# Sixteen gate column blocks moved behind the mLSTM into a segment of their own, in a one-core streaming-encoder layer

## The chip, the core and the metric

The kernel runs on one core of one Trainium2 chip. The metric is device microseconds of one execution. The kernel before took 1607.51 us (median of 3 runs, 1606.27 to 1607.71).

## The reference

One trunk layer of a hybrid encoder, for a prompt of 1024 tokens and a sample stream of 32 tokens (1056 token columns together), all in float32. What matters here, shortened:

```python
h = rmsnorm(x, g_mix) * (1 + sc1) + sh1
u = h @ w_in                                   # 1024 x 5640
qa, ka, va, qm, km, vm, om, ip, fp, ga, gm = split(u)
ya = band_attention(qa, ka, va, rel_bias)      # 8 heads x 64, own 64-frame chunk and 8 before it
q_m, k_m = silu(causal_conv4(qm, km))
hm = mlstm_chunkwise(q_m, k_m, vm, ip, fp)     # 4 heads x 128, running matrix memory
ym = head_rmsnorm(hm) * sigmoid(om)
merged = sigmoid(ga) * (ya @ w_br_att) + sigmoid(gm) * (ym @ w_br_mlstm)
x = x + gt1 * (merged @ w_out)
x = x + gt2 * ((silu(g) * up) @ w_down)        # after a second modulated norm
```

The merge gates `ga` and `gm` are 2 x 1024 columns of the one input projection. They are used first in the merge, after both branches are done.

## The kernel before

**The products.** TensorE holds a 128x128 block of weights and streams token columns. The 1056 columns are cut in three tiles of 352. A product of float32 accuracy is made of three passes (`PASSES`): weights and activations are each split into a high and a low part. So one 128-column block of `w_in` over one tile (`unit`, L458) is 8 k-blocks times 3 passes, 24 matmuls of 128x352, and a block of three tiles is 72. Each weight block comes by DMA (512 KB, `wraw`), ACT copies its high part (L424) and POOL or DVE subtracts for the low part (L425): POOL as long as the second mLSTM has not begun, DVE from then on (`hm_n[1]` in `weight`).

**The blocks of the input projection** are the `segs` list, worked through in order: for each of four head pairs a key, a value and a query block (`b_qkv`), then the mLSTM's values and convolution inputs (`vm_block`, `conv_block`), its output gates (`om_block`) and the sixteen merge gate blocks (`gate_block`). A gate block is 72 matmuls, three copies out of PSUM on ACT (L677) and one store of 528 KB to a scratch tensor in HBM (`g_d`, L678). The merge reads it back.

**Work beside the blocks.** A segment can name a generator (`attention(hp)`, `mlstm(pr)`, `branch_operands`) that is run beside its blocks. `unit` calls `side.tick()` after every second k-block, so one tick is 6 matmuls and a block of three tiles is 12 ticks. A job started with so many steps and so many ticks takes steps/ticks of a step at each tick; a remainder is drained at the segment's end:

```python
ticks = sum(4 * run.w[2] for run in blocks)
delay = 13 if i >= 5 else 0
job = side.start(gen(), steps, ticks - delay - 4, delay)
```

The order of instructions on TensorE, VectorE (DVE), ScalarE (ACT) and GpSimd (POOL) is the order in which this program writes them; nothing is reordered later. Only SyncE (SP), which issues the DMAs, is ordered by a scheduler.

**One attention step** (`attention`, 22 steps a head pair, one item a step: a head and 128 queries against up to 640 keys): PE transposes the weights of the item before last (L774, into the one `psT` buffer), makes the scores (L747, into the one `psS` buffer) and the values of the item three back (L805, one `psV` buffer for two items). DVE adds the bias and takes the extreme (L761), makes the low part of the transposed weights (L786), the reciprocal (L766) and, after two items, two sums out of `psV` (L812, L813). ACT takes the exponential (L762), copies the transposed weights (L781) and the first value sum (L811). POOL scales the weights (L767). The first step of head pairs 1 to 3 makes the low parts of the queries on DVE (`low_queries`, L643).

**One mLSTM iteration** is two steps (`first` and `second`, 9 blocks of tokens for two heads): PE's scores and transposes (L1107, L1109), its products with the memory, for the memory and for the output (L1137, L1140, L1142). On DVE: `scaled` (L1171), `weigh` (L1125), the memory update (L1151), the sum (L1154), three small ones (L1158 to L1160), and the decay weights (L1113). ACT squares (L1163), POOL takes the root (L1165, L1166), and `scaled` of the next iteration needs that root.

**A second job**, `ada_rest`, runs beside all segments from the second on: 160 steps over 495 ticks, most of them one DVE instruction of 128x512 (L1229).

Of the kernel before, what the change touches and what calls it, by code (L numbers as in the profile page):

```python
# [139 lines left out]
def hybrid_stream_step(  # L140
# [37 lines left out]
    def slot(shape, dt=F32):  # L178
        return slots.tile(shape, dt, tag="s", name=nm("s"))

    def tmpt(shape=(P, T), dt=F32):
        return tmp.tile(list(shape), dt, tag="t", name=nm("t"))

    def mmt():
        return mm.tile([P, 512], F32, tag="mm", name=nm("mm"))
# [236 lines left out]
    def split_to(dst, src, eng=dve):  # L422

        act.activation(dst[:, 0], src, AF.Copy)  # L424
        eng.tensor_tensor(dst[:, 1], src, f(dst[:, 0]), op=ALU.subtract)  # L425
# [25 lines left out]
    def unit(w, w0, xt, lo, hi, last=True):  # L451

        wt = W.use(w)
        pt = mmt()
        n = len(xt)
        for k in range(n):
            for q, (a, b) in enumerate(PASSES):
                pe.matmul(pt[:, :hi - lo], wt[(w0 + k) // 4][:, a, (w0 + k) % 4], xt[k][:, b, lo:hi],  # L458
                          start=(k == 0 and q == 0), stop=(k == n - 1 and q == 2))
            if k % 2 == 0 and k:  # L460
                side.flush(1)
            if k % 2 == 1:
                side.tick()
        if last:
            W.used(w)
        return pt[:, :hi - lo]
# [86 lines left out]
    def w_cols(c0, home=None):  # L553
        return weight([w_in[:, c0:c0 + P]], KD, 3, home)
# [115 lines left out]
    def gate_block(g, j):  # L670
        w = w_cols((GA, GM)[g] + j * P)

        def run():
            raw = tmpt()
            for lo, hi in TILES:
                pt = unit(w, 0, hs, lo, hi)
                act.activation(raw[:, lo:hi], pt, AF.Copy)  # L677
            sp.dma_start(g_d[2 * j + g], raw)  # L678
        run.w = w
        return run  # L680
# [155 lines left out]
    ATT_STEPS = 22  # L836
# [364 lines left out]
    ML_STEPS = 2 * (NB + 3) + 2  # L1201
# [56 lines left out]
    def om_block(b):  # L1258
        w = w_cols(OM + b * P)

        def run():
            if b % 2 == 0:
                om[b // 2] = slot([P, 2, T])
            for lo, hi in TILES:
                pt = unit(w, 0, hs, lo, hi)
                act.activation(om[b // 2][:, b % 2, lo:hi], pt, AF.Copy)
        run.w = w
        return run

    def branch_operands():  # L1270
        for b in range(4):
            o = om[b // 2][:, b % 2]
            act.activation(o, o, AF.Sigmoid)
            dve.tensor_tensor(o, o, hm_n[b // 2][:, b % 2], op=ALU.mult)
            y = slot([P, 2, T], F32R)
            yield
            split_to(y, o)
            ym.append(y)
            yield
        if "ym" in dbg:  # L1280
            for h in range(MH):
                sp.dma_start(dbg["ym"][h], om[h // 2][:, h % 2])
        for b in range(4):
            raw = tmpt()
            sp.dma_start(raw, ya_d[b])
            y = slot([P, 2, T], F32R)
            split_to(y, raw)
            ya.append(y)
            yield

    BR_STEPS = 12

    def chain(*gens):
        for g in gens:
            yield from g


    def b_qkv(hp):
        return [k_block(hp), v_block(hp), q_block(hp)]
# [3 lines left out]
    def b_gates(a, b):  # L1303
        return [gate_block(g, j) for g, j in gates[a:b]]

    def mix(a, b):

        out = []
        for i, x in enumerate(a):
            out.append(x)  # L1310
            out += b[i * len(b) // len(a):(i + 1) * len(b) // len(a)]
        return out
# [7 lines left out]
    def conv_rows():  # L1320
        yield
        pt = mmt()
        pe.transpose(pt[:48, :P], ncv, ident)
        ncr = tmpt((48, P))
        dve.tensor_copy(ncr, pt[:48, :P])
        sp.dma_start(new_conv_p[0, 0].rearrange("j (r c) -> (j r) c", c=P), ncr[0:24])
        sp.dma_start(new_conv_s[0, 0].rearrange("j (r c) -> (j r) c", c=P), ncr[24:48])

    nothing = lambda: None
    segs = [  # L1330
        (nothing, b_qkv(0), None, 0),
        (nothing, mix(b_qkv(1), b_gates(0, 2)), lambda: attention(0), ATT_STEPS),
        (nothing, mix(b_qkv(2), b_gates(2, 4)), lambda: attention(1), ATT_STEPS),
        (conv_state, b_qkv(3) + b_gates(4, 8), lambda: attention(2), ATT_STEPS),
        (mlstm_setup, [vm_block(0), conv_block(0), conv_block(4), conv_block(1), conv_block(5)],
         lambda: attention(3), ATT_STEPS),
        (open_mls, [vm_block(1), conv_block(2), conv_block(6), conv_block(3), conv_block(7)],
         lambda: mlstm(0), ML_STEPS),
        (nothing, [om_block(b) for b in range(4)] + b_gates(8, 16),
         lambda: chain(mlstm(1), conv_rows(), branch_operands()), ML_STEPS + BR_STEPS + 3),  # L1340
    ]

    for _, blocks, _, _ in segs:
# [431 lines left out]
    for pi, tiles in enumerate(parts):  # L1775
        if pi == 1:
            job = side.start(second_norm(parts[0]), 15, 50)
        for j in range(KD):
# [21 lines left out]
            a, b = tiles[0][0], tiles[-1][1]  # L1800
# [494 lines left out]
```

## Time and profile before

| what | value |
|---|---|
| timed runs | 1606.27, 1607.51, 1607.71 us; median 1607.51 |
| profiled execution | span 1604.4 us (its time outside the span is not listed apart) |
| PE busy | 1576.2 us, 98% of the span |
| PE's weight loads (PEld) | 1554.8 us, 97% |
| DVE, ACT, POOL busy | 1135.5, 786.2, 445.3 us |
| granted TensorE clock | 0.999 |
| `wraw` from `w_in` | 38 DMAs of 512 KB, 4.0 us from issue to landing |
| `g_d` stores | 16 DMAs of 528 KB, 3.9 us |

The page gives busy time by engine, and groups of instructions by source line. Consecutive matmuls overlap in the records, so the distance between starts says more than the length of one. In a list of instructions in order of time a row is: start in us, length in us, engine, line, operation, what it writes and reads, how many instructions the row joins, and in brackets the idle time before it with what ended it. A table by stretches gives each engine's busy us and, in brackets, its instructions. The segments of the kernel before lie in the span about like this: first products to 72 us, first head pair's blocks to 90, then attention of head pair 0 (90 to 171), 1 (171 to 256), 2 (256 to 360) and 3 (360 to 465), the first mLSTM pair (465 to 570), and om blocks, gates 8 to 15, the second mLSTM pair and the branch operands (570 to 720).

### The profile page before, as it was taken

What the parts mean: (1) busy time and instruction counts of PE and PEld (TensorE: products, weight loads), DVE (VectorE), ACT (ScalarE), POOL (GpSimd) and SP (SyncE); (2) the same over time, 40 slices, a digit from 0 to 9 for tenths busy, and PEclk for the clock granted to TensorE, in tenths of its full rate; (3) what the DMA queues carried; (4) which work ended last, traced back from release to release, by engine and by line L of the source; (5) the groups of instructions that cost most, each with busy time, mean ns of one, the idle gap of its engine ahead of it and who ended that gap; (6) DMA issues with size and microseconds to landing.
All of it is one profiled execution on the core that took longest, in us unless ns stands there. A gap on an engine that the chain in (4) does not pass through costs nothing.

```text
span 1604.4 us, 27406 instructions
## 1 busy us (share of the span) xinstructions
PE 1576.2 (98%) x10256; PEld 1554.8 (97%) x10256; DVE 1135.5 (71%) x2185; ACT 786.2 (49%) x1747; POOL 445.3 (28%) x477
## 2 busy tenths in 40 slices
PE   7999999999999999999999999999999999999997
PEld 6989999999999999999999999999999999999997
DVE  7766564646776855556654699988888986799754
ACT  3665463544455644444443655554544444545443
POOL 2344243433332411000012100566565650000001
PEclk9999999999999999999999999999999999999999
DMA  9823323232222232675353311313222227427453
GB/s 362 273 77 91 97 82 102 88 122 86 67 80 80 69 95 69 121 276 168 121 153 113 106 54 48 100 55 105 81 79 94 67 82 252 135 79 250 135 156 126
DMA packets 210414, 192.45 MB, mean 120 GB/s; under 512 B 10706, under 2 KB 180618, under 8 KB 209258
## 3 DMA queue, kind: packets, MB, share of 16 engines
q1 hardware_dynamic: 205386, 187.82, 37.4%
q10 hardware_dynamic: 4640, 2.82, 0.6%
q8 instruction: 81, 1.33, 0.4%
q14 instruction: 51, 0.42, 0.1%
q0 software_dynamic: 256, 0.06, 0.0%
HBM read 152.19 MB, written 41.63 MB: 121 GB/s over the span
## 4 chain that ended last, share of the span: by engine, by line
PE 88%; DVE 5%; DMA 3%; ACT 2%; issue 1%; SPq 0%; ACTq 0%; POOL 0%; DVEq 0%; POOLq 0%
PE mm L458 39%; PE psb L1843 18%; PE mm L1843 10%; PE mm L2246 3%; PE mm L906 3%; PE psb L2246 2%; PE psV L805 2%; PE psb L2089 2%; PE psS L747 1%; DMA s<-in_w_ada_dram 1%; PE psT L774 1%; PE mm L2089 1%; DMA wraw<-in_w_in_dram 1%; DMA t<-in_x_sample_dram 1%; DVE s L390 1%
## 5 line engine op out<-in xcount | busy, mean ns | idle before, releaser
L458 PE MATMUL mm<-s,wsp 128*128 128x352 f32 x4104 | 689.1, 324 | 0.0
L458 PEld LDWEIGHTS mm<-s,wsp 128*128 128x128 f32 x4104 | 656.9, 188 | 2.0 <-issue 0.4
L425 DVE TENSOR_TENSOR wsp<-wraw,wsp 128x512 fp32r<-128x512 f32 (+1 forms) x280 | 234.9, 855 | 120.0 <-ACT wsp L424 118.0
L1843 PE MATMUL psb<-s,wsp 128*128 128x352 f32 x1611 | 271.7, 322 | 1.5 <-DVE wsp L425 0.8
L424 ACT ACTIVATE wsp<-wraw 128x512 fp32r<-128x512 f32 x336 | 199.5, 617 | 141.5 <-PE psb L1843 44.0
L1843 PEld LDWEIGHTS psb<-s,wsp 128*128 128x128 f32 x1611 | 260.6, 188 | 2.1 <-DVE wsp L425 1.1
L1843 PE MATMUL mm<-s,wsp 128*128 128x352 f32 x933 | 159.3, 322 | 0.0
L1843 PEld LDWEIGHTS mm<-s,wsp 128*128 128x128 f32 x933 | 151.2, 188 | 0.5 <-DVE wsp L425 0.5
L767 POOL TENSOR_SCALAR st<-st,mx 128x640 f32<-128x640 f32 (+5 forms) x72 | 55.7, 774 | 184.8 <-DVE mx L766 170.5
L1229 DVE SCALAR_TENSOR_TENSOR t<-wa,cmix,t 128x512 f32<-128x512 f32 x112 | 89.1, 801 | 15.0 <-DMA wa<-in_w_ada_dram 14.6
L425 POOL TENSOR_TENSOR wsp<-wraw,wsp 128x512 fp32r<-128x512 f32 x56 | 75.8, 1374 | 49.4 <-ACT wsp L424 47.9
L762 ACT ACTIVATE st<-st,mx 128x640 f32<-128x640 f32 (+5 forms) x72 | 47.9, 666 | 71.6 <-DVE mx L761 70.3
L761 DVE CUSTOM_DVE_ANT_0 st<-psS,bias 128x640 f32<-128x640 f32 (+5 forms) x72 | 44.3, 616 | 46.1 <-PE psS L747 33.2
L1790 POOL TENSOR_TENSOR t<-t,sl 128x352 f32<-128x352 f32 x19 | 18.3, 961 | 185.3 <-DMA wraw<-in_w_out_dram 130.8
L781 ACT ACTIVATE pT<-psT 128x640 fp32r<-128x640 f32 (+3 forms) x80 | 38.6, 493 | 63.1 <-PE psT L774 47.7
L2158 POOL TENSOR_TENSOR fst<-fst 128x1 f32<-128x1 f32 (+1 forms) x6 | 1.2, 192 | 236.6 <-ACT t L2151 236.6
L786 DVE TENSOR_TENSOR pT<-psT,pT 128x640 fp32r<-128x640 f32 (+3 forms) x80 | 43.9, 557 | 22.5 <-ACT pT L781 22.3
L1452 POOL TENSOR_TENSOR wraw<-wraw,raw 128x512 f32<-128x512 f32 x33 | 55.8, 1702 | 0.9
L906 PE MATMUL mm<-s,s 128*128 128x264 f32 (+3 forms) x432 | 54.8, 283 | 0.0
L2246 PE MATMUL mm<-s,wsp 128*128 128x352 f32 x330 | 54.4, 324 | 0.0
L2246 PEld LDWEIGHTS mm<-s,wsp 128*128 128x128 f32 x330 | 53.1, 188 | 0.0
L1452 POOL TENSOR_TENSOR spare<-wraw 128x512 f32<-128x512 f32 x11 | 16.5, 1496 | 130.0 <-DMA wraw<-in_w_gate_up_dram 122.4
(396 smaller groups left out, 2561.3 us busy)
## 6 DMA issues: line engine op xcount, KB each, us to landing
wraw<-in_w_in_dram SPq DMA_DIRECT2D x38, 512.0 KB, 4.0
wraw<-in_w_gate_up_dram SPq DMA_DIRECT2D x33, 512.0 KB, 3.8
wa<-in_w_ada_dram SPq DMA_DIRECT2D x64, 256.0 KB, 2.9
wraw<-in_w_down_dram SPq DMA_DIRECT2D x32, 512.0 KB, 4.0
a_d<-t SPq DMA_DIRECT2D x22, 528.0 KB, 2.8
g_d<-t SPq DMA_DIRECT2D x16, 528.0 KB, 3.9
x<-xres SPq DMA_DIRECT2D x16, 528.0 KB, 6.7
t<-g_d SPq DMA_DIRECT2D x16, 528.0 KB, 5.4
```

Of the source, the lines that this page charges most:

```text
L424: act.activation(dst[:, 0], src, AF.Copy)
L425: eng.tensor_tensor(dst[:, 1], src, f(dst[:, 0]), op=ALU.subtract)
L458: pe.matmul(pt[:, :hi - lo], wt[(w0 + k) // 4][:, a, (w0 + k) % 4], xt[k][:, b, lo:hi], start=(k == 0 and q == 0), stop=(k == n - 1 and q ...
L761: dve.tensor_tensor_reduce(so, sv, bi, -1.0, 3.0e38, ALU.add, ALU.min, mx[:n, 1:2])
L762: act.activation(st[:n, :w], st[:n, :w], AF.Exp, bias=mx[:n, 1:2], scale=-1.0, accum_out=mx[:n, 2:3])
L767: pool.tensor_scalar(st[:n, :w], st[:n, :w], mx[:n, 3:4], 1.0, op0=ALU.mult, op1=ALU.mult)
L906: pe.matmul(pt[:n, :wd], hs[k][:, a, i * P:i * P + n], whl[b][:, k, :wd], start=(k == 0 and q == 0), stop=(k == KD - 1 and q == 2))
L1229: dve.scalar_tensor_tensor(ac[:, c], wa, cmix[:, c, k:k + 1], ac[:, c], op0=ALU.mult, op1=ALU.add)
L1452: self.eng.tensor_tensor(a(dst), a(x), a(y), op=op)
L1843: pe.matmul(acc, wt[:, a, k], x[k][:, b], start=(start and not onto and k == 0 and q == 0), stop=(stop and k == 3 and q == 2), skip_group_ ...
L2089: pe.matmul(acc, wt[k // 4][:, u, k % 4], piece_of[k, i][:, v], start=(k == 0 and q == 0), stop=(k == KP - 1 and q == 2))
L2246: pe.matmul(acc, wt[(k - k0) // 4][:, u, (k - k0) % 4], piece_of[k, 2][:, v], start=(k == 0 and q == 0), stop=(k == NF - 1 and q == 2))
```

## The change

The gates leave the segments of attention 0, 1 and 2 (two, two and four blocks) and the last segment (eight). A new last segment holds all sixteen, and `branch_operands` runs beside them. Attention 0 to 2 keep their 22 steps but have 36 ticks (three blocks) in place of 60, 60 and 84. The second mLSTM pair and the convolution rows keep their 29 steps but have the 48 ticks of the four om blocks; before, they shared 144 ticks with `branch_operands`. Total ticks are the same, and so is the arithmetic. The weights of the first eight gates are now split on DVE instead of POOL.

```diff
@@ -1329,15 +1329,16 @@
     segs = [
         (nothing, b_qkv(0), None, 0),
-        (nothing, mix(b_qkv(1), b_gates(0, 2)), lambda: attention(0), ATT_STEPS),
-        (nothing, mix(b_qkv(2), b_gates(2, 4)), lambda: attention(1), ATT_STEPS),
-        (conv_state, b_qkv(3) + b_gates(4, 8), lambda: attention(2), ATT_STEPS),
+        (nothing, b_qkv(1), lambda: attention(0), ATT_STEPS),
+        (nothing, b_qkv(2), lambda: attention(1), ATT_STEPS),
+        (conv_state, b_qkv(3), lambda: attention(2), ATT_STEPS),
         (mlstm_setup, [vm_block(0), conv_block(0), conv_block(4), conv_block(1), conv_block(5)],
          lambda: attention(3), ATT_STEPS),
         (open_mls, [vm_block(1), conv_block(2), conv_block(6), conv_block(3), conv_block(7)],
          lambda: mlstm(0), ML_STEPS),
-        (nothing, [om_block(b) for b in range(4)] + b_gates(8, 16),
-         lambda: chain(mlstm(1), conv_rows(), branch_operands()), ML_STEPS + BR_STEPS + 3),
+        (nothing, [om_block(b) for b in range(4)] + b_gates(0, 0),
+         lambda: chain(mlstm(1), conv_rows()), ML_STEPS + 3),
+        (nothing, b_gates(0, 16), branch_operands, BR_STEPS),
     ]
```

How this moves instructions, at the two places of which the prediction speaks. First PE in attention of head pair 0, second head, full width (640 keys), in the kernel before. `st` are the weights to transpose, `s_699` the keys, `mm` is the PSUM tile of a block's unit:

```order
L774 MATMUL psT_1609<-ident,st_1530 128x128 x5
L747 MATMUL psS_1617<-s_699,s_731 128x320
L747 MATMUL psS_1617<-s_699,s_735 128x320
L747 MATMUL psS_1617<-s_699,s_731 128x320
L747 MATMUL psS_1617<-s_699,s_735 128x320
L805 MATMUL psV_1586<-pT_1568,s_793 128x256 x4
L458 MATMUL mm_1641<-s_449,wsp_1253 128x352 x3
L458 MATMUL mm_1641<-s_497,wsp_1253 128x352 x3
L458 MATMUL mm_1641<-s_531,wsp_1253 128x352 x3
L458 MATMUL mm_1641<-s_558,wsp_1253 128x352 x3
L774 MATMUL psT_1654<-ident,st_1575 128x128 x5
```

Two ticks (12 matmuls) stand between one step and the next here, three (18) between others. The changed kernel's PE in the same head of the same attention:

```order
L774 MATMUL psT_1393<-ident,st_1338 128x128 x4
L747 MATMUL psS_1400<-s_699,s_731 128x320
L747 MATMUL psS_1400<-s_699,s_735 128x320
L747 MATMUL psS_1400<-s_699,s_731 128x320
L747 MATMUL psS_1400<-s_699,s_735 128x320
L805 MATMUL psV_1412<-pT_1359,s_793 128x256 x3
L458 MATMUL mm_1427<-s_449,wsp_1119 128x352 x3
L458 MATMUL mm_1427<-s_497,wsp_1119 128x352 x3
L774 MATMUL psT_1435<-ident,st_1365 128x128 x5
```

One tick (6 matmuls) stands between these two steps; steps with one and with two ticks behind them alternate. Second, PE in the second mLSTM pair of the kernel before, between the scores' end of one iteration (L1177 is the transpose of the output of three iterations back) and its `second` step:

```order
L1177 MATMUL mm_6855<-ident,num_6709 128x128 x2
L458 MATMUL mm_6834<-s_531,wsp_6622 128x352 x3
L458 MATMUL mm_6834<-s_558,wsp_6622 128x352 x3
L458 MATMUL mm_6834<-s_585,wsp_6623 128x352 x3
L458 MATMUL mm_6834<-s_611,wsp_6623 128x352 x3
L458 MATMUL mm_6834<-s_638,wsp_6623 128x352 x3
L458 MATMUL mm_6834<-s_675,wsp_6623 128x352 x3
L1137 MATMUL psT_6882<-C_6805,s_5651 128x129
L1137 MATMUL psT_6882<-C_6805,s_6088 128x129
L1140 MATMUL psV_6883<-s_5268,kw_6759 128x129 x2
L1142 MATMUL psT_6882<-s_5268,W_6755 128x129 x2
```

Three ticks stand between the two steps. The same in the changed kernel:

```order
L1177 MATMUL mm_6005<-ident,num_5897 128x128 x2
L458 MATMUL mm_5981<-s_531,wsp_5731 128x352 x3
L458 MATMUL mm_5981<-s_558,wsp_5731 128x352 x3
L1137 MATMUL psT_6019<-C_5958,s_4878 128x129
L1137 MATMUL psT_6019<-C_5958,s_5319 128x129
L1140 MATMUL psV_6020<-s_4497,kw_5930 128x129 x2
L1142 MATMUL psT_6019<-s_4497,W_5926 128x129 x2
```

One tick stands between them, so a whole iteration of two steps has about two ticks (12 matmuls) in place of six (36).

## The prediction

> **What bounds the kernel now.** I read the page's busy shares first, then a table by stretches, the waits, and lists of instructions in order of time. The page:
>
> ```profile
> span 1604.4 us, 27406 instructions
> PE 1576.2 (98%) x10256; PEld 1554.8 (97%) x10256; DVE 1135.5 (71%) x2185; ACT 786.2 (49%) x1747; POOL 445.3 (28%) x477
> ```
>
> PE bounds, with 28 us not busy in 1604.4. What the moved blocks could win or lose must be read in their stages. The table by stretches (stretch, its length, then busy us of PE, PEld, DVE, ACT, POOL, the granted clock, the DMA share, GB/s): attention 0, 1, 2, the second mLSTM's stage with its gates, and four us of the start.
>
> ```profile
> 90.00:171.00 81.00, 78.59 (x525) 75.25 (x523) 47.86 (x123) 43.69 (x104) 29.24 (x36) 1.00 0.30 88
> 171.00:256.00 85.00, 84.39 (x566) 81.75 (x566) 51.22 (x127) 45.18 (x107) 32.10 (x41) 1.00 0.30 91
> 256.00:360.00 104.00, 103.46 (x691) 101.64 (x690) 57.07 (x134) 49.40 (x116) 40.69 (x46) 1.00 0.33 102
> 570.00:760.00 190.00, 190.00 (x1237) 188.44 (x1237) 99.55 (x215) 84.80 (x208) 12.16 (x24) 1.00 0.52 149
> 12.00:16.00 4.00, 2.84 (x24) 2.38 (x22) 3.29 (x8) 3.97 (x8) 0.40 (x1) 1.00 1.04 360
> ```
>
> In the three attentions PE is idle for 270.00 - 266.44 = 3.6 us in all, in the mLSTM's stage for nothing. That is the most that a thinner mixture there could win. DVE works 156 of 270 us (58%). What PE waits for, from 70 to 760 us, names the resources that are nearest to binding:
>
> ```profile
> PE psT L774 <- DVE pT L786: 1.3, 2, 1.0
> PE psT L774 <- POOL wsp L425: 0.9, 1, 0.9
> PE psS L747 <- DVE mx L761: 0.9, 2, 0.4
> PE psV L805 <- DVE t L813: 0.8, 4, 0.2
> ```
>
> Totals in us, times, longest: small, but all of them are attention's single PSUM buffers. So I ask how much less than today's distance between two steps these buffers allow.
>
> **The change part by part.** First, what moves for nothing. Ticks, matmuls, steps, evictions and stores are the same in number. The sixteen gate blocks alone need no side work: by this row a product matmul takes (7.01 - 0.33)/41 = 0.163 us, a tick of six 0.98 and a block 11.7 us,
>
> ```profile
> 251.35 7.01 PE L458 MATMUL mm<-s,wsp 128*128 128x352 f32 x42
> ```
>
> while ACT has three evictions and four splits at most for it, and DVE its splits (a gate's low parts go from POOL to DVE, 1.29 us each there; even at that price four are 5.2 us) beside `ada_rest`, a quarter of the 11.7. The groups of attention 1's stretch (count, busy us, mean ns, idle before):
>
> ```profile
> L643 DVE TENSOR_TENSOR s<-t,s 64x1056 fp32r<-64x1056 f32 x2 | 2.5, 1250 | 0.0
> L573 DVE TENSOR_TENSOR s<-mm,s 64x352 fp32r<-64x352 f32 x6 | 3.1, 522 | 1.7 <-ACT kf L571 1.6
> L424 ACT ACTIVATE wsp<-wraw 128x512 fp32r<-128x512 f32 x10 | 5.7, 622 | 0.0
> L677 ACT ACTIVATE t<-mm 128x352 f32<-128x352 f32 x6 | 2.8, 462 | 6.2 <-PE mm L458 5.7 <-PE psS L747 0.5
> L425 POOL TENSOR_TENSOR wsp<-wraw,wsp 128x512 fp32r<-128x512 f32 x12 | 15.2, 1292 | 19.3 <-ACT wsp L424 19.2
> ```
>
> ACT: 3 x 0.46 + 4 x 0.62 = 3.9 us of 11.7. The sixteen weight loads and sixteen stores on SP's queue: 16 x (512 + 528) KB in 16 x 11.7 us are 91 GB/s, beside the roughly 90 of the table's stages; 360 GB/s were moved at 12 us. They are hidden; without that cover each late block would cost about its transfer's 4 us. The merge starts behind the same number of matmuls. I take 0 for this segment.
>
> Second, attention 0 to 2. What was spread over 60, 60 and 84 ticks now has 36. Steps stand alternately one and two ticks apart. PE in order of time, attention 0, full-width items:
>
> ```profile
> 146.27 0.71 PE L774 MATMUL psT<-ident,st 128*128 128x128 f32 x5
> ...
> 147.87 2.09 PE L458 MATMUL mm<-s,wsp 128*128 128x352 f32 x12
> 149.79 0.71 PE L774 MATMUL psT<-ident,st 128*128 128x128 f32 x5
> ...
> 150.95 0.83 PE L805 MATMUL psV<-pT,s 128*128 128x256 f32 x5
> 151.62 3.05 PE L458 MATMUL mm<-s,wsp 128*128 128x352 f32 x18
> 154.51 0.71 PE L774 MATMUL psT<-ident,st 128*128 128x128 f32 x5
> ```
>
> The step from 149.79 to 154.51 lasts 4.72 us, of which 18 x 0.163 = 2.93 are products; its own matmuls take 1.79. With one tick it lasts 2.77 for PE, with two 3.75, a pair 6.52. DVE in the same time:
>
> ```profile
> 149.93 0.42 DVE L812 TENSOR_TENSOR t<-psV,t 64x256 f32<-64x256 f32 x1 [0.24 <-ACT t L811]
> 150.38 0.42 DVE L813 TENSOR_TENSOR t<-psV,t 64x256 f32<-64x256 f32 x1
> 151.23 0.82 DVE L761 CUSTOM_DVE_ANT_0 st<-psS,bias 128x640 f32<-128x640 f32 x1 [0.43 <-PE psS L747]
> 151.98 0.82 DVE L786 TENSOR_TENSOR pT<-psT,pT 128x640 fp32r<-128x640 f32 x1
> 153.05 0.16 DVE L766 RECIPROCAL mx<-mx 128x1 f32<-128x1 f32 x1 [0.25 <-ACT st L762]
> 153.13 0.73 DVE L1229 SCALAR_TENSOR_TENSOR t<-wa,cmix,t 128x512 f32<-128x512 f32 x1
> ```
>
> The low part (L786) that frees `psT` ends at 152.80, 3.01 us after its step began. A one-tick step offers 2.77, so the next transposes wait 0.24. `psV` is free when L813 ends, 150.80, 4.53 us after the step at 146.27 in which its pair of items ended; the next values would start 2.77 + 1.16 (150.95 - 149.79) = 3.93 us after it, so 0.60 of waiting, in every second step. Half at 0.24 and half at 0.60 is 0.42 a full-width one-tick step, on a quiet DVE and ACT.
>
> They are not quiet: DVE's gaps of today are where `ada_rest` (160 steps in 495 ticks, 0.73 us, so 0.24 a tick) and the splits fit. ACT has 10 splits in the stretch's 88 ticks (0.07 a tick), POOL 12 (0.18). Together 0.49 a tick, each a delay of up to that in a chain without slack; I take 0.4, near the upper end, because the chain runs over all three engines. So 0.8 for each of some 7 full-width one-tick steps an attention (bounds: 0.3 and 1.3), and 0.3 for each of 4 narrow ones, whose tiles are half as long: 3 x (7 x 0.82 + 4 x 0.3) = 20.8 us. In attention 1 and 2 the first scores stand one tick behind `low_queries` in place of two or three; its two instructions are 2.5 us against 0.98 and the first step's own work, some 0.8 of waiting each (bounds 0.3 and 1.5), 1.6. The idle of today, 3.6 us, is partly the same waits, so 2 come off: **+20**, bounds 3 x (7 x 0.3) - 3.6 = +3 and 3 x (7 x 1.3 + 4 x 0.6) + 3 = +37.
>
> DVE's mean does not forbid it: 156 us of work less 31 moved `ada_rest` steps (96 ticks x 160/495) x 0.73 = 133 in 270 - 96 x 0.98 = 176 us, 76%. The waits come from the order, not from a full engine.
>
> Third, the second mLSTM. An iteration had six ticks, now two. PE around one:
>
> ```profile
> 595.32 0.61 PE L1137 MATMUL psT<-C,s 128*128 128x129 f32 x4
> ...
> 596.57 3.14 PE L458 MATMUL mm<-s,wsp 128*128 128x352 f32 x18
> ...
> 600.34 3.13 PE L458 MATMUL mm<-s,wsp 128*128 128x352 f32 x18
> 603.31 0.60 PE L1137 MATMUL psT<-C,s 128*128 128x129 f32 x4
> ```
>
> 603.31 - 595.32 = 7.99 us with 36 product matmuls (5.87), so 2.12 of its own; with twelve, 1.96 + 2.12 = 4.08. The loop that carries one iteration to the next, over DVE, ACT and POOL, from the scaling of one to that of the next:
>
> ```profile
> 596.49 0.60 DVE L1171 TENSOR_SCALAR num<-num,dn 128x128 f32<-128x128 f32 x2
> ...
> 597.85 0.42 DVE L1154 TENSOR_TENSOR num<-num,psT 128x258 f32<-128x258 f32 x1
> ...
> 598.69 0.17 DVE L1160 RECIPROCAL dn<-dn 128x2 f32<-128x2 f32 x1
> ...
> 598.95 0.40 ACT L1163 ACTIVATE sq<-num,dn 128x128 f32<-128x128 f32 x1 [1.47 <-DVE dn L1160]
> ...
> 600.06 0.68 POOL L1165 TENSOR_SCALAR dn<-dn 128x2 f32<-128x2 f32 x1 [7.12 <-ACT sq L1163]
> ...
> 600.83 0.69 POOL L1166 TENSOR_TENSOR dn<-dn,mhalf 128x2 f32<-128x2 f32 x1
> ...
> 601.56 0.61 DVE L1171 TENSOR_SCALAR num<-num,dn 128x128 f32<-128x128 f32 x2 [0.86 <-POOL dn L1166]
> ```
>
> DVE stands at the last row for POOL's root, with the weights (L1125) and the memory update queued behind, for which PE's next `second` step waits. The loop takes 601.56 - 596.49 = 5.07 us against PE's 4.08: 0.99 x 8 intervals = **+8**. Bounds: 0.6 an interval where one of the two `ada_rest` steps' delays falls away (+5), 1.6 with one more 0.6 split in it (+13).
>
> **Sum:** 0 + 20 + 8 = +28 on the profiled 1604.4, 1632. The median of the runs is 3.1 us above that span, so the time is 1607.5 + 28, **1635 us**.
>
> **The rivals.** *Chains compound* (slower still). The rows from 149.93 to 153.13 + 0.73 show DVE's work for one item end to end, 3.93 us with its short waits on PE and ACT. If an item cannot be taken faster than that, a pair takes 7.86 against PE's 6.52: 1.34 x 21 full-width pairs = 28, 12 narrow at 0.6 = 7, first steps 2, mLSTM 13: +50, 1657. For it: the brackets 0.24, 0.43 and 0.25 lie in series. Against it: `ada_rest` does not stand in every item.
>
> *Only one place pays.* Attention's waits stay at 0.3 a full-width step (about +6 with the narrow ones) and the mLSTM's output tile runs ahead for part of its nine iterations (+4): +10, 1617. For it: PE is never idle in the mLSTM's stage today, and the three iterations' lag of the output shows room.
>
> *Not slower.* The mechanism is the average: DVE's work for a pair is 2 x (0.82 + 0.82 + 0.16) + 0.84 + 0.73 = 5.17 us, 5.95 with 1.5 of the key parts (0.52), both below 6.52. If PE's two-tick steps let DVE catch up what the one-tick step left over, no wait arises, and waits of now, which stand where blocks of gates bring extra splits, go: at most the 3.6 idle us, 1604. It decides if the waits behind one-tick steps are under 0.1 us. Against it: the buffers `psT` and `psV` are single, so a catch-up comes too late for the step that waited.
>
> *The clock.* If short idle times in 108 ticks' worth of dense attention took the granted clock to a half, 108 x 0.98 = 106 us more would come on top, 1741. Against it: the stretch from 12 us has PE busy in 2.84 of 4.00 us and clock 1.00. [...] The trace so far does not bear it out.
>
> **How the numbers follow.** Forecast 0.59 (own range 1620 to 1650: 28 less 15 or plus 15 where not all bounds meet), compounding 0.17, one place 0.12, not slower 0.10, the clock 0.02. The range 1612 to 1660 takes in the forecast, the one-place case and most of compounding; it leaves out the not-slower case, the clock and what goes beyond 50. About 3.2 us (0.2%) is the least that this measurement tells from no change; the not-slower case, -4 to 0, splits into 0.04 faster and 0.06 the same; all else is slower, 0.90.
>
> **What would show it.** In the changed profile PE's idle time in attention 0 to 2 is some 20 us more than today's 3.6, put down to L786 (`psT`), L813 (`psV`) and L761 (`psS`); attention 1 and 2 show a wait on L643 at the start. In the second mLSTM some 8 us wait at L1142 or L1107 for DVE behind POOL's L1166, and iterations are 5.1 us apart. The gate segment has PE without gaps at 11.7 us a block, and the clock stays at 1.00. I am wrong if these waits are not there, if PE waits for `wraw` in the gate segment, or if the merge starts later by more than the sum.

## The result, and the profile after

The changed kernel takes 1666.54 us (median of 4 runs, 1665.99 to 1667.27) against 1607.24 us: a ratio of 1.037, with a 95% interval of 1.0356 to 1.0385. That is 59.3 us slower. The forecast was 1635 and the range ended at 1660: the direction was right, the size was not, and less than half of the loss was foreseen. One execution of e1_att_only and one of e11_444 below took about 3156 us, nearly twice the others; the medians are given without these, and the cause is open.

The page of the changed kernel:

```profile
span 1664.3 us, 27421 instructions
PE 1599.4 (96%) x10256; PEld 1568.1 (94%) x10256; DVE 1140.5 (69%) x2201; ACT 784.8 (47%) x1747; POOL 422.8 (25%) x461
```

PE is not busy for 64.9 us now (28 before) and its busy time has grown by 23 us, although it does the same 10256 matmuls. Busy time that grows at equal work already says that something other than waiting is in it.

To place the loss I use landmarks that both kernels have: the first copy of the mLSTM's values out of PSUM (L914, the end of attention 2's stage), the `om` blocks' copies (L1266), and the gates' copies (L677). First the kernel before, then the changed one; in the grouped rows the two times at the end are the first and the last start:

```profile
365.19 0.39 ACT L914 ACTIVATE s<-mm 128x256 f32<-128x256 f32 x1 [1.84 <-PE mm L906]
L1266 ACT ACTIVATE s<-mm x12: 443/465/483, 559.5 to 610.4; 128x352 f32<-128x352 f32 x12
```

```profile
319.48 0.39 ACT L914 ACTIVATE s<-mm 128x256 f32<-128x256 f32 x1 [0.82 <-PE mm L906]
L1266 ACT ACTIVATE s<-mm x12: 442/464/472, 515.9 to 589.8; 128x352 f32<-128x352 f32 x12
L677 ACT ACTIVATE t<-mm x48: 445/464/467, 593.6 to 776.0; 128x352 f32<-128x352 f32 x48
589.40:776.90 187.50, 187.50 (x1174) 187.44 (x1173) 68.63 (x99) 52.75 (x95) 4.63 (x6) 1.00 0.48 158
```

The last row is the gates' own stage: 187.5 us for sixteen blocks, 11.72 each, PE without a gap and at full clock. Eight blocks fewer (93.8 us) should bring L914 to 271.4; it stands at 319.5. So attention 0 to 2 lost **48 us**. The first `om` copy should stand at 465.7 and is at 515.9: 50 up to there, so attention 3 and the first mLSTM lost **2**. The rest of the 59.9 us in span, **9.7**, is the second mLSTM's.

Where PE waits from 72 to 320 us in the changed kernel (totals in us, times, longest):

```profile
PE psT L774 <- DVE pT L786: 12.0, 15, 2.3
PE psS L747 <- DVE mx L761: 10.8, 6, 2.3
PE psV L805 <- DVE t L813: 7.8, 12, 2.7
PE psT L774 <- DVE mx L766: 1.1, 2, 0.6
PE psT L774 <- POOL st L767: 0.9, 1, 0.9
```

With two small ones of 0.4 these are 33.4 us in 39 waits; in the same part of the kernel before, 3.7 us in 11. Three things stand out that the prediction did not have in this form.

**The start of an attention.** All six waits for L761 (10.8 us) stand behind the first and second scores of attention 0, 1 and 2. Attention 1, in order of time, all engines, with rows left out:

```profile
161.55 0.33 PE L747 MATMUL psS<-s,s 128*128 128x128 f32 x2
...
162.84 2.50 POOL L425 TENSOR_TENSOR wsp<-wraw,wsp 128x512 fp32r<-128x512 f32 x2
165.28 0.14 POOL L714 MEMSET bias<- 64x64 f32 x1
...
165.46 0.29 DVE L761 CUSTOM_DVE_ANT_0 st<-psS,bias 128x128 f32<-128x128 f32 x1 [3.05 <-POOL bias L714]
...
165.81 0.50 PE L747 MATMUL psS<-s,s 128*128 128x256 f32 x2 [1.96 <-DVE mx L761]
...
167.27 1.06 DVE L573 TENSOR_TENSOR s<-mm,s 64x352 fp32r<-64x352 f32 x2 [0.79 <-ACT s L568]
168.36 0.75 DVE L1229 SCALAR_TENSOR_TENSOR t<-wa,cmix,t 128x512 f32<-128x512 f32 x1
169.15 0.42 DVE L761 CUSTOM_DVE_ANT_0 st<-psS,bias 128x256 f32<-128x256 f32 x1
...
169.63 1.01 PE L747 MATMUL psS<-s,s 128*128 128x384 f32 x2 [2.17 <-DVE mx L761]
...
170.44 3.72 PE L458 MATMUL mm<-s,wsp 128*128 128x352 f32 x12
```

The scores are ready at 161.9, but the bias tile is not: its memset (L714) stands on POOL behind a weight split of 2.50 us. DVE waits 3.05 us for it, PE 1.96 for DVE. For the next scores the key's low parts and the second job stand ahead of L761, and PE waits 2.17 more.

**The clock.** The last row above is twelve products in 3.72 us. The twelve at 109.89 us, where the granted clock is 1.00, took 2.09. Stretches of 3.41 us, laid 0.3 us behind the points at which the granted clock changes, so that 0.96 and 0.54 stand where a change falls inside a stretch (length, busy us of PE, PEld, DVE, ACT, POOL, granted clock, DMA share, GB/s):

```profile
89.02:92.43 3.41, 1.68 (x9) 1.31 (x9) 2.40 (x7) 1.41 (x4) 1.07 (x4) 0.96 0.52 129
92.43:95.84 3.41, 2.61 (x9) 2.62 (x10) 1.87 (x9) 1.59 (x5) 0.48 (x1) 0.50 0.08 25
95.84:99.26 3.42, 3.42 (x14) 3.16 (x13) 0.40 (x2) 0.38 (x1) 0.74 (x1) 0.54 0.26 77
...
191.42:194.83 3.41, 1.48 (x14) 1.51 (x15) 2.24 (x7) 1.87 (x4) 2.11 (x2) 0.96 0.22 48
194.83:198.24 3.41, 3.41 (x17) 3.19 (x17) 1.83 (x5) 1.08 (x5) 0.63 (x3) 0.54 0.88 284
...
256.27:259.68 3.41, 1.79 (x14) 1.54 (x12) 2.59 (x7) 1.46 (x4) 0.22 (x1) 1.00 0.26 77
```

In this trace the granted clock is 1.00 or 0.50, and from 85 to 332 us its twelve changes lie 3.41 us or a multiple of it apart: it stood at 0.50 for 3.41 us three times and for 6.83 us three times. The six stretches at full clock with PE busy for 1.68 us or less were each followed by one at half clock; those with 1.79 us or more were not. A slow stretch was followed by another where PE was busy in it for 1.31 to 2.71 us, and by a full one where it was busy for 3.41. No wait of PE in attention 0 to 2 was longer than 2.7 us. Behind the single hole of 1.85 us at the start of attention 3, which fell whole into one stretch (1.56 us busy), the clock went to 0.50 as well. Two waits of like length came out differently here: the 2.33 us ahead of 193.35 us fell into one stretch (1.48 us busy) and the clock dropped, the 2.32 us ahead of 117.53 were shared by two (2.3 and 2.2 us busy) and it did not.

The nine slow stretches from 92 to 332 us hold 27.1 us of PE's busy time and, at a clock of 0.50, cost at most half of that, 13.6 us; two in the second mLSTM (577 to 584 us) hold 5.9 and cost at most 2.9. Products alone start 0.293 us apart in a slow stretch (171 to 174 us) and 0.16 in the gates' stage, so of their time 45% is lost; at that rate the eleven stretches cost 14.9 us and not 16.5. The kernel before has none from 60 to 800 us.

**What stands ahead on DVE in the body of an attention.** The longest wait there comes once in attention 0 and 1 alike:

```profile
113.38 1.06 DVE L573 TENSOR_TENSOR s<-mm,s 64x352 fp32r<-64x352 f32 x2 [0.56 <-ACT kf L571]
114.45 1.33 DVE L1229 SCALAR_TENSOR_TENSOR t<-wa,cmix,t 128x512 f32<-128x512 f32 x1
115.82 0.82 DVE L761 CUSTOM_DVE_ANT_0 st<-psS,bias 128x640 f32<-128x640 f32 x1
116.57 0.82 DVE L786 TENSOR_TENSOR pT<-psT,pT 128x640 fp32r<-128x640 f32 x1
```

```profile
117.53 0.74 PE L774 MATMUL psT<-ident,st 128*128 128x128 f32 x5 [2.32 <-DVE pT L786]
```

One step meets the key's low parts and the second job together, and L1229 takes 1.33 us, with weight splits on POOL beside it from 113.95 to 116.91 us, in place of 0.73. The step's bias and low part come that much later.

The sum for attention 0 to 2: 29.7 us more waiting; 28 more waits, each reckoned with the overlap of matmuls that it breaks, 3.4 to 4.8 (an estimate: rows of 12, 18 and 42 products last 2.09, 3.05 and 7.01 us in the kernel before, n x 0.163 plus 0.12 to 0.17 us); and the slow clock of eight of the nine stretches, 10.7 to 11.9. Together 44 to 46 of the measured 48.

### The profile page after: what moved, and what is told of

Its sections match the earlier page's. It is cut to its first block, busy times and chain, and to the rows that moved or that the text cites. A ratio compares the mean times of both kernels' runs of the same rounds, so it can differ in the third digit from the quotient of the medians.

```text
span 1664.3 us, 27421 instructions
## 1 busy us (share of the span) xinstructions
PE 1599.4 (96%) x10256; PEld 1568.1 (94%) x10256; DVE 1140.5 (69%) x2201; ACT 784.8 (47%) x1747; POOL 422.8 (25%) x461
## 3 DMA queue, kind: packets, MB, share of 16 engines
q8 instruction: 81, 1.33, 0.3%
## 4 chain that ended last, share of the span: by engine, by line
PE 81%; DVE 7%; DMA 4%; ACT 4%; issue 2%; POOL 2%; SPq 0%; ACTq 0%; DVEq 0%; POOLq 0%
PE mm L458 36%; PE psb L1844 17%; PE mm L1844 10%; PE mm L2247 3%; PE mm L906 3%; PE psb L2247 2%; PE psb L2090 2%; DVE st L761 1%; DMA xres<-s 1%; PE psS L747 1%; DMA s<-in_w_ada_dram 1%; PE psT L774 1%; PE psV L805 1%; PE mm L2090 1%; ACT st L762 1%
## 5 line engine op out<-in xcount | busy, mean ns | idle before, releaser
L458 PE MATMUL mm<-s,wsp 128*128 128x352 f32 x4104 | 698.6, 327 | 0.0
L458 PEld LDWEIGHTS mm<-s,wsp 128*128 128x128 f32 x4104 | 665.8, 191 | 2.2 <-issue 0.4
L425 DVE TENSOR_TENSOR wsp<-wraw,wsp 128x512 fp32r<-128x512 f32 (+1 forms) x296 | 246.5, 851 | 163.1 <-ACT wsp L424 161.2
L1844 PE MATMUL mm<-s,wsp 128*128 128x352 f32 x933 | 159.2, 322 | 0.0
L1844 PEld LDWEIGHTS mm<-s,wsp 128*128 128x128 f32 x933 | 151.2, 188 | 0.4 <-DVE wsp L425 0.3
L767 POOL TENSOR_SCALAR st<-st,mx 128x640 f32<-128x640 f32 (+5 forms) x72 | 50.1, 695 | 168.4 <-DVE mx L766 140.0
L1229 DVE SCALAR_TENSOR_TENSOR t<-wa,cmix,t 128x512 f32<-128x512 f32 x112 | 83.7, 766 | 10.4 <-DMA wa<-in_w_ada_dram 10.1
L677 ACT ACTIVATE t<-mm 128x352 f32<-128x352 f32 x48 | 22.3, 464 | 125.6 <-PE mm L458 117.2
L761 DVE CUSTOM_DVE_ANT_0 st<-psS,bias 128x640 f32<-128x640 f32 (+5 forms) x72 | 44.4, 616 | 46.4 <-PE psS L747 26.6
L425 POOL TENSOR_TENSOR wsp<-wraw,wsp 128x512 fp32r<-128x512 f32 x40 | 53.1, 1348 | 31.9 <-ACT wsp L424 31.0
L747 PE MATMUL psS<-s,s 128*128 128x320 f32 (+2 forms) x192 | 46.3, 350 | 12.7 <-DVE mx L761 12.7
L2247 PE MATMUL mm<-s,wsp 128*128 128x352 f32 x330 | 54.4, 324 | 0.0
L906 PEld LDWEIGHTS mm<-s,s 128*128 128x128 f32 (+1 forms) x432 | 53.5, 185 | 0.5
```

Source lines behind the costliest of these rows:

```text
L747: pe.matmul(sc[:, o:o + b - a], x[:, hh, q0:q0 + P], kt[:, hh, k0 + a:k0 + b], start=(i == 0), stop=(i == 1))
L761: dve.tensor_tensor_reduce(so, sv, bi, -1.0, 3.0e38, ALU.add, ALU.min, mx[:n, 1:2])
L767: pool.tensor_scalar(st[:n, :w], st[:n, :w], mx[:n, 3:4], 1.0, op0=ALU.mult, op1=ALU.mult)
L906: pe.matmul(pt[:n, :wd], hs[k][:, a, i * P:i * P + n], whl[b][:, k, :wd], start=(k == 0 and q == 0), stop=(k == KD - 1 and q == 2))
L1229: dve.scalar_tensor_tensor(ac[:, c], wa, cmix[:, c, k:k + 1], ac[:, c], op0=ALU.mult, op1=ALU.add)
L1844: pe.matmul(acc, wt[:, a, k], x[k][:, b], start=(start and not onto and k == 0 and q == 0), stop=(stop and k == 3 and q == 2), skip_group_ ...
```

## The experiments

### Each place by itself

```diff
# e1_att_only, against the changed kernel
-        (nothing, [om_block(b) for b in range(4)] + b_gates(0, 0),
-         lambda: chain(mlstm(1), conv_rows()), ML_STEPS + 3),
-        (nothing, b_gates(0, 16), branch_operands, BR_STEPS),
+        (nothing, [om_block(b) for b in range(4)] + b_gates(8, 16),
+         lambda: chain(mlstm(1), conv_rows(), branch_operands()), ML_STEPS + BR_STEPS + 3),
+        (nothing, b_gates(0, 8), None, 0),
# e2_mlstm_only, against the kernel before
-        (nothing, [om_block(b) for b in range(4)] + b_gates(8, 16),
-         lambda: chain(mlstm(1), conv_rows(), branch_operands()), ML_STEPS + BR_STEPS + 3),
+        (nothing, [om_block(b) for b in range(4)],
+         lambda: chain(mlstm(1), conv_rows()), ML_STEPS + 3),
+        (nothing, b_gates(8, 16), branch_operands, BR_STEPS),
```

> Only the first eight gates move (attention 0 to 2 get 36 ticks each); the last eight stay beside the second mLSTM pair. By the landmarks of the two profiles (the second half's first vm copy, L914, stands at 319.5 us in place of 365.2 with eight gates of 11.69 us fewer ahead of it) attention 0 to 3 carry +50 of the +59. Theory (two places that add up): +49 us, 1654 to 1660. Rival (one place makes the other worse, or part of the loss sits in the gates' own segment): under +40 or over +57.

> Only the last eight gates move; attention 0 to 2 keep their eight. Theory: the second mLSTM pair in 48 ticks costs +10 us by the landmarks (my prediction had 8), 1614 to 1620. Rival (the mLSTM costs only in the company of the dense attention): under +4.

Measured against 1606.34 us: e1_att_only 1655.18 (ratio 1.0304, 1.0287 to 1.0321), 48.8 us more; e2_mlstm_only 1617.06 (1.0066, 1.0051 to 1.0081), 10.7 more. Together 59.5 for 59.3 of the whole change. The two places add up, and nothing is left for the gates' own segment.

### POOL's queue at the start of an attention

```diff
# e3_bias_dve, against the changed kernel
-        pool.memset(bt[0:64, 576:640], -BIG)
-        pool.memset(bt[64:128, 0:64], -BIG)
+        dve.memset(bt[0:64, 576:640], -BIG)
+        dve.memset(bt[64:128, 0:64], -BIG)
```

> The changed kernel with the two 64x64 memsets of each bias tile (L714, L715) on DVE in place of POOL. Theory (each attention starts with a hole because DVE's first L761 stands for a memset behind POOL's query rows and weight split, 3.05 and 2.47 us in two of them): the first hole of each of the four starts goes (1.67, 1.96, 2.26 and 1.85 us), and the clock no longer falls to a half behind it in three (about 7 us long each): 14 us less than the changed kernel, between 9 and 20 less. Rival (the holes are DVE's own, with the query's low parts and the key parts ahead): at most 3 us less and the clock falls as before.

1655.27 us (1.03, 1.0283 to 1.0317), 11.3 less than the changed kernel, inside the band. PE's waits for L761 fall from 12.7 to 4.8 us (attention 3's start included). The first hole goes in attention 1, 2 and 3 but stays in attention 0 (2.04 us), for another reason, two rows of its DVE:

```profile
86.43 3.11 DVE L643 TENSOR_TENSOR s<-t,s 64x352 fp32r<-64x352 f32 x2
...
89.94 0.29 DVE L761 CUSTOM_DVE_ANT_0 st<-psS,bias 128x128 f32<-128x128 f32 x1
```

The queries' low parts take 1.55 us each there, beside POOL's weight split. The clock part of the expectation held by a third: of nine slow stretches in the attentions six are left, some of them in new places, as the other holes now fall into other stretches. The waits for L761 that went (7.9 us), less 1.5 more for POOL (L767), and the slow stretches that went (3.2 to 3.6) make up most of the gain.

### The second job

```diff
# e4_ada_gates, against the changed kernel
-        if i == 1:
-            ada = side.start(ada_rest(), ADA_STEPS, 495)
+        if i == 7:
+            ada = side.start(ada_rest(), ADA_STEPS, 184)
```

> The changed kernel with the whole second job (ada_rest, 160 steps) beside the gates' own segment, none beside attention and mLSTM. Theory (the second job's DVE instructions stand in chains that have no slack, the prediction's 0.24 us a tick): the waits in attention fall by about a third and with them some of the slow clock, 12 us less than the changed kernel (6 to 18 less), the gates' segment stays at 187 us. Rival 1 (chain of a step alone sets the waits): within 3 us of the changed kernel. Rival 2 (DVE in the gates' segment, four splits of 0.86 and ten of 0.73 in each 11.7 us, becomes late): more time than the changed kernel, with PE waiting for the weights' low parts there.

1676.41 us (1.0435, 1.042 to 1.0451), 10 more than the changed kernel, but two things are in it. Up to the mLSTM the theory held: the first L914 copy stands at 306.8 in place of 319.5, 12.7 us earlier, and the waits for L786 fall from 12.3 us. Waits are not all of it: four slow stretches are left up to there in place of eight, worth about 5 to 6 us. Two rows of PE's waits:

```profile
PE mm L1243 <- DVE t L1238: 20.3, 8, 4.7
...
PE psT L774 <- DVE pT L786: 7.2, 13, 1.0
```

The first row is most of the loss: in the gates' segment PE stands eight times for the second job's own transposes, and five slow stretches stand at three of these holes. From the first L677 copy to the last it is 212.9 us (573.8 to 786.7) in place of 182.4. The DVE there is not full, as rival 2 had it (busy for 127.6 of the 212.9 us); it waits for its weights, for which there are two tiles (`wa`), to land:

```profile
617.71 1.42 DVE L1229 SCALAR_TENSOR_TENSOR t<-wa,cmix,t 128x512 f32<-128x512 f32 x2 [3.76 <-DMA wa<-in_w_ada_dram]
```

So neither the dense nor the empty place takes this job for nothing at that rate.

### The clock

```diff
# e5_filler, against the changed kernel
+            if i in (1, 2):
+                pt = mmt()
+                for _ in range(8):
+                    pe.matmul(pt[:, :352], kt[:, 0, 0:P], kt[:, 0, 0:352], start=True, stop=True)
             if i < n:
                 sts[i] = scores(items[i])
```

> The changed kernel with eight product-sized matmuls on TensorE (128x352, about 1.3 us, into a PSUM tile that nobody reads) ahead of the second and the third scores of each attention, where PE stands idle for 1.36 to 2.26 us. Nothing else changes; they do no work of the layer. Theory (the clock is set for stretches of 3.41 us, to a half after a stretch with PE busy for less than half of it; seven of the nine slow stretches of attention follow these holes): they stay at full clock, and (2.61 + 3.42 + 1.31 + 3.41 + 2.71 + 3.42 + 3.41) / 2 = 10 us go, 6 to 13 less than the changed kernel, though PE does 64 matmuls more. Rival (the clock falls for another reason, or the slow stretches lie beside other waits and cost nothing): no less time, or up to 64 x 0.163 = 10 us more.

1660.93 us (1.034, 1.0324 to 1.0355): 5.6 us less than the changed kernel, just short of the band; 6.7 less in the profiled spans, and 4.6 if each is taken against the kernel before of its own round (1606.23 and 1607.24). PE does 64 matmuls (10 us) of useless work more. Of nine slow stretches in the attentions two are left (253 and 304 us). The bound in the expectation, less than half of a stretch, is read off the changed kernel's trace (1.68 of 3.41 us and less); in this run one stretch with 1.52 us (184.45 to 187.87 us, laid by its slow stretches) was followed by full clock. The rest of the expected 10 us went where the fillers overfill the holes:

```profile
PE psS L747 <- DVE mx L761: 2.7, 4, 1.0
...
PE mm L826 <- DVE s L573: 2.1, 2, 1.1
```

L826 is the filler itself. The holes now hold 10.4 us of fillers and 2.7 + 2.1 of waits, 15.2 us where 12.7 were idle, so 2.5 more. A kernel that does more work on the engine that bounds it became faster, and the clock is what changed in its trace.

### How much slack a step needs

```diff
# e6_half, against the kernel before
-        (nothing, mix(b_qkv(1), b_gates(0, 2)), lambda: attention(0), ATT_STEPS),
-        (nothing, mix(b_qkv(2), b_gates(2, 4)), lambda: attention(1), ATT_STEPS),
-        (conv_state, b_qkv(3) + b_gates(4, 8), lambda: attention(2), ATT_STEPS),
+        (nothing, b_qkv(1)[:2] + b_gates(0, 1) + b_qkv(1)[2:], lambda: attention(0), ATT_STEPS),
+        (nothing, b_qkv(2)[:2] + b_gates(1, 2) + b_qkv(2)[2:], lambda: attention(1), ATT_STEPS),
+        (conv_state, b_qkv(3) + b_gates(2, 6), lambda: attention(2), ATT_STEPS),
...
+        (nothing, b_gates(6, 8), None, 0),
```

> The kernel before with one gate block taken from attention 0 and one from attention 1 (48 ticks in place of 60, so that steps stand two ticks apart), both put behind the last segment; the other fourteen stay. Theory (a two-tick step of 3.75 us hides the 3.01 us in which psT comes free, and the holes stay short enough for the clock): +3 us on the kernel before, 0 to +6, clock at 1.00. Rival (the loss grows in proportion to the blocks taken away: 49 us for eight): +12 us.

1615.65 us (1.0058, 1.0043 to 1.0073), 9.4 more: neither the threshold (0 to 6) nor full proportion (12), though nearer to the latter. The granted clock stays at 1.00 from 60 to 330 us. PE's waits:

```profile
PE psT L774 <- DVE pT L786: 7.3, 8, 1.4
PE psS L747 <- DVE mx L761: 3.3, 4, 1.2
```

The first scores of the two attentions wait (L761), and two-tick steps wait as well. Ahead of the wait of 1.36 us that ends at 109.48 us stand the key's low parts (1.06 us) and the second job (1.31), as ahead of the longest wait of the changed kernel. The quiet chain of 3.01 us is not what has to fit into a step, but that chain with whatever stands ahead of it on DVE.

### Who makes the weights' low parts

```diff
# e7_om_pool, against e2_mlstm_only (late is filled when the last segment begins)
# e8_split_dve, against the changed kernel
-  pool if (W.done or home is slots) and not hm_n[1] else dve
+  pool if (W.done or home is slots) and not late else dve        # e7_om_pool
+  pool if home is slots and not hm_n[1] else dve                 # e8_split_dve
```

> The kernel with only the last eight gates moved (e2_mlstm_only), with the weights' low parts made on POOL as long as the second mLSTM runs, in place of DVE. Theory (in the dense mLSTM PE's longest wait, 3.05 us for L1125, stands behind a weight split of 1.71 us on DVE): 3 us less than e2_mlstm_only (1.5 to 6 less). Rival (my prediction's loop through POOL's root L1165, L1166 binds): the splits stand ahead of the root on POOL, 4 us more than e2_mlstm_only or worse.

> The changed kernel with all weights' low parts made on DVE, also beside attention, so that POOL has only its own parts of attention. Theory (DVE's queue is what the one-tick steps wait for; 8 splits of 0.85 us come onto it in each 12 ticks of a block at most): +8 us on the changed kernel, +3 to +15. Rival (POOL's splits are the delay: they stand ahead of the bias and of L767, and a DVE instruction beside one took 1.33 us in place of 0.73): 8 us less than the changed kernel or more.

e7_om_pool: 1617.27 us (1.0068, 1.0053 to 1.0083), as e2_mlstm_only; neither theory nor rival, though its runs lie 4.4 us apart, so that a gain of 1.5, the least expected, is not excluded. PE's two kinds of wait there hardly change (L1125 2.7 to 2.3, L1171 2.8 to 3.1 us). The split has left DVE, but not the path: beside it on POOL, DVE's scaling (L1173 in this run, L1171 in the others) takes 2.52 us in place of 0.6.

```profile
590.96 2.50 POOL L425 TENSOR_TENSOR wsp<-wraw,wsp 128x512 fp32r<-128x512 f32 x2
591.03 2.52 DVE L1173 TENSOR_SCALAR num<-num,dn 128x128 f32<-128x128 f32 x2 [1.70 <-POOL dn L1168]
```

e8_split_dve: 1662.78 (1.0351, 1.0333 to 1.0368), 3.8 less than the changed kernel (2.7 against the kernel before of its own round), between both. Its waits show why, with the starts better and the body worse:

```profile
PE psT L774 <- DVE pT L786: 16.8, 17, 3.0
PE psV L805 <- DVE t L813: 8.2, 14, 2.6
PE psS L747 <- DVE mx L761: 4.0, 4, 1.4
PE psS L747 <- DVE s L643: 3.8, 2, 2.3
```

### The other way round

```diff
# e9_more_early, against the kernel before (with the memsets on DVE as in e3_bias_dve)
-        (nothing, mix(b_qkv(1), b_gates(0, 2)), lambda: attention(0), ATT_STEPS),
-        (nothing, mix(b_qkv(2), b_gates(2, 4)), lambda: attention(1), ATT_STEPS),
-        (conv_state, b_qkv(3) + b_gates(4, 8), lambda: attention(2), ATT_STEPS),
+        (nothing, mix(b_qkv(1), b_gates(0, 3)), lambda: attention(0), ATT_STEPS),
+        (nothing, mix(b_qkv(2), b_gates(3, 6)), lambda: attention(1), ATT_STEPS),
+        (conv_state, b_qkv(3) + b_gates(6, 10), lambda: attention(2), ATT_STEPS),
...
-        (nothing, [om_block(b) for b in range(4)] + b_gates(8, 16),
+        (nothing, [om_block(b) for b in range(4)] + b_gates(10, 16),
# e11_444, against the kernel before (memsets on POOL), the same lines
+        (nothing, mix(b_qkv(1), b_gates(0, 4)), lambda: attention(0), ATT_STEPS),
+        (nothing, mix(b_qkv(2), b_gates(4, 8)), lambda: attention(1), ATT_STEPS),
+        (conv_state, b_qkv(3) + b_gates(8, 12), lambda: attention(2), ATT_STEPS),
...
+        (nothing, [om_block(b) for b in range(4)] + b_gates(12, 16),
```

> The other way round: the kernel before with three, three and four gate blocks beside attention 0, 1 and 2 (in place of two, two and four) and six in the last segment, and the bias tiles' memsets on DVE. Theory (each block beside attention buys slack for its chains; PE is idle for 3.6 us there in the kernel before, and the second mLSTM has slack to give with 120 ticks): 2 us less than the kernel before, 0 to 4 less. Rival (the remaining idle is not from spacing, or the last segment now loses what attention wins): within 1 us of the kernel before, or slower.

> The kernel before with only the bias tiles' memsets on DVE. Theory (in the kernel before the first scores stand two or three ticks behind the low parts of the queries, so POOL's queue is mostly over by then): 0 to 1.5 us less than the kernel before. Rival (POOL's queue holds up the starts there too): 3 us less or more.

> The kernel before with four gate blocks beside each of attention 0, 1 and 2 (84 ticks each) and four in the last segment, where the second mLSTM then has 96 ticks; the memsets stay on POOL. In e9_more_early PE's idle in the three attentions had fallen from 3.6 to 1.3 us. Theory (only idle that is left can be won): 0 to 1.5 us less than e9_more_early, so 5 to 7.5 less than the kernel before. Rival (the second mLSTM's stage in 96 ticks begins to wait): 2 us more than e9_more_early or worse, with PE waits on L1125 or L1171.

e9_more_early takes 1600.79 us against 1606.56, a ratio of 0.9967 (0.9955 to 0.9979), faster than both kernels by more than expected; e10_before_bias 1606.92 (1.0002, 0.9993 to 1.0011), no change, so the memsets are not what wins; e11_444 1600.15 against 1606.60 (0.9961, 0.9948 to 0.9974), 6.45 less and inside its band, but not to be told from e9_more_early. All of PE's waits from 60 to 800 us that e9_more_early has left, where the kernel before had 5.1 us:

```profile
PE psT L774 <- DVE pT L786: 1.6, 2, 1.2
```

3.5 us of the 5.8 are waits that went; eleven waits fewer at the estimated 0.17 make at most 1.9 more. The last segment gives up these blocks for nothing down to 96 ticks for the second mLSTM and the branch operands; it was 48 that cost. Behind that there is no more to win here, since PE waits for 1.0 us in e11_444 from 60 to 800 us.

## Why the prediction was wrong, by its own steps

The sum was 28 us and the spans differ by 59.9, so 32 were missing. The slow clock, which had no term in the sum, is 15 to 16.5 of them; the starts of the attentions, sized at 1.6, are 9.2 more, and 1.85 more in attention 3; the broken overlap behind each wait, which had no term either, is 4 to 5.5 by the estimate above.

**The gates' own segment, 0.** Right: 187.5 us at 11.72 a block, no waits, and e1_att_only and e2_mlstm_only leave nothing for it. DVE's splits and the stores are hidden there.

**The body of attention, 20.8.** Nearly right as a sum, not as a picture, so in part by luck. Without the six waits at the starts PE waits 33.4 - 10.8 = 22.6 us in attention 0 to 2. But this is not 0.82 us in each full-width one-tick step: it is a few waits of 0.2 to 1.0, one of 1.6, and one of 2.3 or more in each attention where several other instructions stand ahead. Two-tick steps, which I took to be free, wait too (e6_half). The term for what stands between (0.4) was the right kind: without the second job 12.7 us go up to the mLSTM, waits and slow clock together (e4_ada_gates).

**The start of an attention, 1.6.** This step failed. I priced L643 against one tick, in attention 1 and 2, and did not follow the other inputs of the first L761: the bias tile's memset, behind POOL's query rows and weight split. The second scores then wait again. 10.8 us in place of 1.6, and a start in attention 0 and, with 1.85 us, in attention 3, that I had at nothing. The wait on L643 that was to show this term is not in the changed kernel's list. e3_bias_dve takes 11.3 us back with a change of engine for two small memsets.

**The clock, a rival at 0.02.** This step failed too, and by more. The rival was dismissed by one row, 2.84 of 4.00 us busy at full clock; that is 71%, and the six stretches ahead of half clock in the changed kernel had PE busy for 1.39 to 1.68 of 3.41 us, 41 to 49%. It was also priced as all or nothing, 106 us, and no run shows that term. It came as eleven stretches and at most 13.6 + 2.9 = 16.5 us by the profile, and e5_filler, which does nothing but keep PE busy in the holes, gets 5.6 us back net of its own 2.5. My terms for waits were added up as if a wait cost its own length; at the starts of the four attentions it cost that and a slow clock for 3.41 or 6.83 us behind it.

**The second mLSTM, +8.** The size was near (10.7 by e2_mlstm_only), the mechanism was not, so the size is luck. The loop of 5.07 us does not set the distance of iterations (starts of the `second` step):

```profile
536.38 0.61 PE L1137 MATMUL psT<-C,s 128*128 128x129 f32 x4
...
540.82 0.61 PE L1137 MATMUL psT<-C,s 128*128 128x129 f32 x4
...
545.41 0.61 PE L1137 MATMUL psT<-C,s 128*128 128x129 f32 x4
...
552.87 0.61 PE L1137 MATMUL psT<-C,s 128*128 128x129 f32 x4
```

They are 4.4, 4.6 and then 7.5 us apart, and one before these 3.9: the loop can stretch over iterations, which fits the output's lag. The loss is one wait of 3.05 us and two at the end of 1.82 and 0.95, at most 2.9 us of slow clock, 0.2 for a short fourth wait and some 0.7 for broken overlap, by the estimate above: 9.6 of the profile's 9.7 at most. Of the two at the end only the second stands for POOL's root. Ahead of the first the root was ready at 572.96, and DVE stood 2.55 us for ACT's copy of a weight and then made its low part in 1.29:

```profile
572.26 0.70 POOL L1166 TENSOR_TENSOR dn<-dn,mhalf 128x2 f32<-128x2 f32 x1
573.32 1.29 DVE L425 TENSOR_TENSOR wsp<-wraw,wsp 128x512 fp32r<-128x512 f32 x2 [2.55 <-ACT wsp L424]
...
574.93 0.60 DVE L1171 TENSOR_SCALAR num<-num,dn 128x128 f32<-128x128 f32 x2
575.41 0.50 PE L1177 MATMUL mm<-ident,num 128*128 128x128 f32 x2 [1.82 <-DVE num L1171]
```

A weight split, of 1.71 us, is also ahead of the 3.05 on DVE, from 546.86 us on, with 2.01 us of standing for ACT's copy before it. e7_om_pool gained nothing by moving it, but there DVE's scaling took 2.52 us beside it on POOL. So the split fits both traces as the cause; no run takes it off both engines, and this stays not shown.

**Compounding, 0.17, 1657,** came nearest in size, but for a reason of its own (every full-width pair at DVE's pace) that the waits do not show. The rivals that were not slower, or slower in one place only, are out: both places lose (e1_att_only, e2_mlstm_only).

Some 2 to 4 us of the attentions' 48 are not put down to anything.

## What to carry to other kernels

Filler work beside a latency-bound job is not spare: its price, where it is removed, is not the wait of a mean step but what stands ahead of the job on every shared queue, and the start of the job, where all its inputs meet, has to be followed input by input. When PE begins to idle in short holes, look at the granted clock too: here six stretches of 3.41 us in which PE was idle for 1.73 to 2.02 us were each followed by 3.41 or 6.83 us at 0.50, which cost at most another 1.7 to 3.1 us. And before moving work out of a place, try moving more in: two to four blocks more beside the attentions made this kernel 0.3 to 0.4% faster than before.

## What the runs showed of the hardware

- The granted clock behind holes: of the 28 full-clock stretches of the changed kernel between 85 and 332 us with PE busy for less than 3.0 us, the six with 1.68 us or less were followed by half clock and the 22 with 1.79 or more were not; all twelve changes there lie a multiple of 3.41 us apart. No sharp bound was shown: in e5_filler a stretch with 1.52 us (184.45 to 187.87 us) was followed by full clock (the five transposes at 188.31 us took 0.73), in e3_bias_dve one with 1.82 (164.58 to 167.99) by half.
- A DVE instruction beside POOL's weight split: L643 on 64x352 took 1.55 us beside a weight split on POOL (e3_bias_dve) and 0.53 without one (e8_split_dve, the same place):

```profile
86.45 1.06 DVE L643 TENSOR_TENSOR s<-t,s 64x352 fp32r<-64x352 f32 x2
```

  In the changed kernel L573, which reads one input from PSUM, kept its 0.53 us beside such a split (the second at 113.38 us). What makes the difference is not shown.
- What a wait of PE between matmuls costs beyond its listed length is an estimate, 0.12 to 0.17 us: in the kernel before, rows of 12, 18 and 42 products last 2.09, 3.05 and 7.01 us, that much more than n x 0.163. No run was made for it alone.
